# A row-normalising, row-doubling kernel: loads and stores in other groups, wide operations, roots on two engines

## The chip, the core and the metric

The kernel runs on one core of one Trainium2 chip. Times are microseconds of that core on the device. The core has a scalar engine (ScalarE, ACT in the profile), a vector engine (VectorE, DVE), a general engine (GpSimd, POOL), a tensor engine that this kernel doesn't use (PE), and a synchronising engine (SyncE, SP) that here only issues transfers. Sixteen DMA engines move the data between the chip's memory (HBM) and the on-chip memory (SBUF).

## What is computed

```python
x = randn(8, 512, 2048)   # float32
gamma = randn(2048)
x_rep = np.repeat(x, 2, axis=1)
rms = np.sqrt((x_rep ** 2).mean(axis=-1, keepdims=True) + 1e-6)
out = (x_rep / rms) * gamma
```

Every row of 2048 numbers is divided by the root of its mean square, multiplied by gamma, and written twice, one copy behind the other. The input is 4096 rows (33.6 MB), the output 8192 rows (67.1 MB).

## The kernel before

The 4096 rows are cut into 8 tiles of 128 partitions with K = 4 rows in each partition. A tile `y` has room for K * R = 8 rows per partition, R = 2: the four input rows are loaded into rows 4 to 7 (`at = K * (R - 1) + k`, line 51), and output row pairs 0-1, 2-3, 4-5, 6-7 are made in place from the front, so that an input row is overwritten only when it has been used. The pool `rows` has three such tiles, 64 KB per partition each. So three tiles can be in the works, and the load of tile i + 3 has to wait for the store of tile i.

For each row of a tile: `square` (line 61) has ACT square it and sum the squares along the way (line 64), and take the root of the mean (line 68); `scale` (line 71) has DVE take the reciprocal (line 73) and multiply row, reciprocal and gamma in one instruction into output row 2k (line 74); `repeat` (line 79) copies that to row 2k + 1, on ACT, or on DVE for the last row of a group (line 80). `compute` (line 82) puts these in an order in which ACT squares row k + 1 while DVE scales row k.

The order is written out by hand, and each engine runs its own instructions in the order in which the program gives them. The order on SP's queue is also that of the program: a `dma_start` that has to wait keeps those behind it waiting too. It is: load 0 in two halves, loads 1 and 2; then store 0, store 1, loads 3 and 4, store 2, store 3, loads 5 and 6, and so on in twos (lines 113 to 116). Tile 7 is loaded, computed and stored in halves (`parts`, line 108). Gamma is brought in by four small transfers from ACT's queue (line 98) and copied to all partitions by POOL (line 101).

Of the kernel before, what the change touches and what calls it, by code (L numbers as in the profile page):

```python
# [1 line left out]

# [4 lines left out]


@with_exitstack
def kernel(  # L10
    ctx: ExitStack,
    tc: tile.TileContext,
    x: bass.AP,
    gamma: bass.AP,
    out: bass.AP,
):
    nc = tc.nc
    P = nc.NUM_PARTITIONS
    f32 = mybir.dt.float32
    Act = mybir.ActivationFunctionType  # L20
    Alu = mybir.AluOpType

    B, S, D = x.shape
    Bo, So, Do = out.shape
    R = So // S
    assert R == 2 and D == Do and B == Bo and So == S * R
    eps = 1e-6
    inv_d = 1.0 / float(D)


    K = 4
    N = B * S
    assert N % (P * K) == 0
    ntiles = N // (P * K)
    x_t = x.rearrange("b s d -> (b s) d").rearrange("(n p k) d -> n p k d", p=P, k=K)
    out_t = out.rearrange("b s d -> (b s) d").rearrange("(n p j) d -> n p (j d)", p=P, j=K * R)

    singles = ctx.enter_context(tc.tile_pool(name="singles", bufs=1))
    rows = ctx.enter_context(tc.tile_pool(name="rows", bufs=3))
    junk = ctx.enter_context(tc.tile_pool(name="junk", bufs=1, space=bass.MemoryType.PSUM))  # L40
    small = ctx.enter_context(tc.tile_pool(name="small", bufs=8))

    ys = []

    def load(i, eng, parts=1):


        y = rows.tile([P, K * R, D], f32, name="y")
        step = K // parts
        for k in range(0, K, step):  # L50
            at = K * (R - 1) + k
            eng.dma_start(out=y[:, at : at + step, :], in_=x_t[i, :, k : k + step, :])  # L52
        ys.append(y)

    def store(i, k0, k1):
        nc.sync.dma_start(  # L56
            out=out_t[i, :, R * k0 * D : R * k1 * D],
            in_=ys[i][:, R * k0 : R * k1, :].rearrange("p j d -> p (j d)"),
        )

    def square(i, k):
        sq = junk.tile([P, D], f32, name="sq")
        ss = small.tile([P, 1], f32, name="ss")
        nc.scalar.activation(  # L64
            out=sq[:], in_=ys[i][:, K * (R - 1) + k, :], func=Act.Square, accum_out=ss[:]
        )
        rms = small.tile([P, 1], f32, name="rms")
        nc.scalar.activation(out=rms[:], in_=ss[:], func=Act.Sqrt, scale=inv_d, bias=eps_t[:])  # L68
        return rms

    def scale(i, k, rms):
        rstd = small.tile([P, 1], f32, name="rstd")
        nc.vector.reciprocal(out=rstd[:], in_=rms[:])  # L73
        nc.vector.scalar_tensor_tensor(  # L74
            out=ys[i][:, R * k, :], in0=ys[i][:, K * (R - 1) + k, :], scalar=rstd[:], in1=gamma_b[:],
            op0=Alu.mult, op1=Alu.mult,
        )

    def repeat(i, k, copy):
        copy(out=ys[i][:, R * k + 1, :], in_=ys[i][:, R * k, :])  # L80

    def compute(i, k0, k1):

        rms = square(i, k0)
        for k in range(k0, k1):
            scale(i, k, rms)
            if k + 1 < k1:
                rms = square(i, k + 1)
                repeat(i, k, nc.scalar.copy)
            else:  # L90
                repeat(i, k, nc.vector.tensor_copy)


    ctx.enter_context(tc.manual_schedule())
    load(0, nc.sync, parts=2)
    gamma_b = singles.tile([P, D], f32, name="gamma_b")
    for c in range(0, D, D // 4):
        nc.scalar.dma_start(
            out=gamma_b[0:1, c : c + D // 4], in_=gamma[c : c + D // 4].partition_broadcast(1)
        )  # L100
    nc.gpsimd.partition_broadcast(out_ap=gamma_b[:], in_ap=gamma_b[0:1, :])  # L101
    eps_t = singles.tile([P, 1], f32, name="eps_t")
    nc.vector.memset(eps_t, eps)  # L103
    load(1, nc.sync)
    load(2, nc.sync)

    for i in range(ntiles):
        parts = 2 if i == ntiles - 1 else 1
        for k in range(0, K, K // parts):
            compute(i, k, k + K // parts)  # L110
            store(i, k, k + K // parts)

        if i % 2 == 1:
            for j in (i + 2, i + 3):
                if j < ntiles:
                    load(j, nc.sync, parts=2 if j + 1 == ntiles else 1)


# [1 line left out]
_INS = ['x', 'gamma']  # L120
_OUTS = [((8, 1024, 2048), 'float32')]


# [23 lines left out]
```

## Time and profile before

| | |
|---|---|
| median of 10 runs | 239.82 us (239.68 to 240.98) |
| the profiled execution's own time | 239.77 us |
| its span, first to last instruction | 238.0 us |
| moved by DMA | 100.69 MB, 423 GB/s over the span |
| DVE, ACT, POOL busy | 90.8, 115.3, 2.5 us |
| DMA queue of loads and stores | 98.5% of 16 engines' span |

The profile is of one execution. A row such as "L74 DVE ... x32 | 75.3, 2352 | 1.2" says that line 74's instructions on DVE were 32, that they took 75.3 us together and 2352 ns each, and that DVE stood idle 1.2 us just before them. The chain of waits is followed back from the last instruction to whatever released it. "SPq" is the issue of a transfer on SP's queue; the time from issue to landing stands under "DMA". The slices cut the span into 40 equal parts, with the busy share of each in tenths.

### The profile page before, as it was taken

How to read it: one execution, taken by the hardware profiler on the slowest of the kernel's cores; microseconds unless marked ns; L12 is line 12 of the kernel's file. 1: busy time of each engine (PE TensorE's matmuls, PEld its weight loads, DVE VectorE, ACT ScalarE, POOL GpSimd, SP SyncE). 2: the span in 40 equal slices, each digit the busy share in tenths (PEclk: the TensorE clock that was granted, in tenths of full speed). 3: DMA queues.
4: the chain of work that ended last, by engine and by line, in shares of the span. 5: the costliest groups of instructions: out<-in, count | busy, mean ns of one | idle time of the engine just before them, and what ended most of it. 6: DMA issues, size and time to landing. Idle time of an engine off the chain costs nothing.

```text
span 238.0 us, 301 instructions
## 1 busy us (share of the span) xinstructions
DVE 90.8 (38%) x74; ACT 115.3 (48%) x121; POOL 2.5 (1%) x5
## 2 busy tenths in 40 slices
DVE  0086977864000084967000007796600009900000
ACT  2699999990000299996000049999400049700000
POOL 0300000000000000000000000000000000000000
DMA  7999998989899999989898999999898999898995
GB/s 262 441 443 441 441 441 352 529 352 518 364 408 430 435 408 436 529 352 529 352 529 352 435 424 464 441 408 474 352 529 352 410 435 531 386 474 364 430 430 242
DMA packets 2746, 100.69 MB, mean 423 GB/s; under 512 B 308, under 2 KB 308, under 8 KB 312
## 3 DMA queue, kind: packets, MB, share of 16 engines
q1 hardware_dynamic: 2736, 100.66, 98.5%
q14 instruction: 2, 0.02, 0.0%
q10 hardware_dynamic: 8, 0.01, 0.0%
HBM read 33.56 MB, written 67.11 MB: 423 GB/s over the span
## 4 chain that ended last, share of the span: by engine, by line
DMA 66%; ACT 15%; DVE 6%; issue 1%; SPq 0%; DVEq 0%
DMA out_dram<-y 40%; DMA y<-in_x_dram 25%; ACT sq L64 7%; ACT y L80 5%; DVE y L74 5%; ACT rms L68 1%; ACT L68 1%; DVE y L80 1%; DVE rstd L73 0%; SPq L52 0%; DVEq L74 0%; SPq L56 0%
## 5 line engine op out<-in xcount | busy, mean ns | idle before, releaser
L64 ACT ACTIVATE sq<-y 128x2048 f32<-128x2048 f32 x32 | 59.9, 1871 | 84.9 <-DMA y<-in_x_dram 84.9
L74 DVE SCALAR_TENSOR_TENSOR y<-y,rstd,gamma_b 128x2048 f32<-128x2048 f32 x32 | 75.3, 2352 | 1.2 <-DVE rstd L73 0.2
L73 DVE RECIPROCAL rstd<-rms 128x1 f32<-128x1 f32 x32 | 5.2, 162 | 115.7 <-ACT rms L68 115.7
L80 ACT COPY y<-y 128x2048 f32<-128x2048 f32 x23 | 43.4, 1888 | 3.7 <-DVE y L74 3.7
L80 DVE COPY y<-y 128x2048 f32<-128x2048 f32 x9 | 11.0, 1227 | 0.3
L68 ACT ACTIVATE rms<-ss,eps_t 128x1 f32<-128x1 f32 x32 | 9.4, 295 | 1.0
L64 ACT ACTIVATION_READ_ACCUMULATOR sq<-y 128x1 f32 x32 | 6.0, 186 | 0.0
L101 POOL PARTITION_BROADCAST gamma_b<-gamma_b x1 | 2.3, 2293 | 8.3 <-DMA gamma_b<-in_gamma_dram 8.3
L64 ACT ACT_TABLE_LOAD x1 | 1.3, 1283 | 2.1 <-issue 2.1
L68 ACT ACT_TABLE_LOAD x1 | 1.3, 1283 | 0.0
L103 DVE MEMSET eps_t<- 128x1 f32 x1 | 0.1, 59 | 0.8 <-PEq L131 0.8
L131 POOL MEMSET const-bfloat16-1.0<- 128x1 bf16 x1 | 0.1, 102 | 0.0
L131 POOL MEMSET const-uint8-127<- 128x1 uint8 x1 | 0.1, 101 | 0.0
L131 POOL MEMSET const-float32-0.0<- 128x1 f32 x1 | 0.1, 98 | 0.2 <-issue 0.2
L131 POOL MEMSET const-float32-1.0<- 128x1 f32 x1 | 0.1, 98 | 0.0
## 6 DMA issues: line engine op xcount, KB each, us to landing
y<-in_x_dram SPq DMA_DIRECT2D x6, 4096.0 KB, 25.0
y<-in_x_dram SPq DMA_DIRECT2D x4, 2048.0 KB, 9.6
out_dram<-y SPq DMA_DIRECT2D x2, 4096.0 KB, 26.8
out_dram<-y SPq DMA_DIRECT2D x7, 31.6
gamma_b<-in_gamma_dram ACTq DMA_DIRECT2D x4, 2.0 KB
```

Of the source, the lines that this page charges most:

```text
L64: nc.scalar.activation(out=sq[:], in_=ys[i][:, K * (R - 1) + k, :], func=Act.Square, accum_out=ss[:])
L68: nc.scalar.activation(out=rms[:], in_=ss[:], func=Act.Sqrt, scale=inv_d, bias=eps_t[:])
L73: nc.vector.reciprocal(out=rstd[:], in_=rms[:])
L74: nc.vector.scalar_tensor_tensor(out=ys[i][:, R * k, :], in0=ys[i][:, K * (R - 1) + k, :], scalar=rstd[:], in1=gamma_b[:], op0=Alu.mult, o ...
L80: copy(out=ys[i][:, R * k + 1, :], in_=ys[i][:, R * k, :])
L101: nc.gpsimd.partition_broadcast(out_ap=gamma_b[:], in_ap=gamma_b[0:1, :])
L103: nc.vector.memset(eps_t, eps)
L131: nc = _bacc.Bacc("TRN2", target_bir_lowering=False, num_devices=1)
```

## The change

The order on SP's queue becomes: first half of load 0, six pieces of gamma, second half of load 0, one more piece of gamma, loads 1 and 2; stores 0, 1, 2; loads 3, 4, 5; stores 3, 4; loads 6, 7; stores 5, 6, 7. Tile 7 is loaded, computed and stored whole, as are all others but the load of tile 0.

Most operations become wide: one instruction for several rows. `square` is now a plain square of several rows, written into output rows that are still free, and `reduce` has DVE sum them. In `mixed`, which does tiles 1, 2, 4, 6 and 7, ACT squares rows 1 to 3 of the tile in one instruction and row 0 with the sum (`total`), DVE reduces the three rows, `root` has POOL multiply, add and take the power -0.5 of all four sums, and DVE does the four multiplications with gamma; the copies are two instructions of two rows, one on ACT and one on DVE (both on ACT for tile 7). While DVE reduces tile i, ACT squares the whole of the next tile (`ahead`), for which DVE then reduces four rows (`row=False`). Tiles 0 and 3 take their roots in halves with ACT's square root and DVE's reciprocal (`root_quick`). Tile 5 is scaled by four ACT instructions, with the root as scale, and one wide multiplication by gamma on DVE; ACT copies all four rows.

Gamma's pieces go to two rows on partitions 0 and 32, and POOL spreads each half to all partitions by itself. ACT's table is loaded by `preload_act_table` ahead of the work.

```diff
-    def load(i, eng, parts=1):
...
+    def load(i, k0, k1):
         nc.sync.dma_start(
...
+            out=ys[i][:, K * (R - 1) + k0 : K * (R - 1) + k1, :], in_=x_t[i, :, k0:k1, :]
+        )
+
+    def store(i):
+        nc.sync.dma_start(out=out_t[i], in_=ys[i].rearrange("p j d -> p (j d)"))
...
+    def total(i, k, ss):
         sq = junk.tile([P, D], f32, name="sq")
...
+            out=sq[:], in_=ys[i][:, x_at + k, :], func=Act.Square, accum_out=ss[:, k : k + 1]
+        )
+
+    def square(i, k0, k1):
+
+        nc.scalar.activation(
+            out=ys[i][:, k0:k1, :], in_=ys[i][:, x_at + k0 : x_at + k1, :], func=Act.Square
+        )
+
+    def reduce(i, k0, k1, ss):
+        nc.vector.tensor_reduce(
+            out=ss[:, k0:k1], in_=ys[i][:, k0:k1, :], op=Alu.add, axis=mybir.AxisListType.X
+        )
+
+    def root(k0, k1, ss):
+        at = ss[:, k0:k1]
+        nc.gpsimd.tensor_scalar(
+            out=at, in0=at, scalar1=inv_d, scalar2=eps, op0=Alu.mult, op1=Alu.add
+        )
+        nc.gpsimd.tensor_tensor(out=at, in0=at, in1=power_t[:, k0:k1], op=Alu.pow)
+
+    def scale(i, k0, k1, rstd):
         for k in range(k0, k1):
...
+            nc.vector.scalar_tensor_tensor(
+                out=ys[i][:, R * k, :], in0=ys[i][:, x_at + k, :], scalar=rstd[:, k : k + 1],
+                in1=gamma_b[:], op0=Alu.mult, op1=Alu.mult,
+            )
+
+    def repeat(i, k0, k1, copy=nc.scalar.copy):
+        y_r = ys[i].rearrange("p (k r) d -> p k r d", r=R)
+        copy(out=y_r[:, k0:k1, 1, :], in_=y_r[:, k0:k1, 0, :])
...
+    cuts = [0, *range(D // 4, D + 1, D // 8)]
...
+    load(0, 0, H)
+    for c0, c1 in zip(cuts[:-2], cuts[1:-1]):
+        gamma_piece(c0, c1)
+    load(0, H, K)
+    gamma_piece(cuts[-2], cuts[-1])
+    for c0 in (0, D // 2):
+        nc.gpsimd.partition_broadcast(out_ap=gamma_b[:, c0 : c0 + D // 2], in_ap=gamma_half(c0))
+    load(1, 0, K)
+    load(2, 0, K)
...
+    def root_quick(k0, k1, ss):
+        at = ss[:, k0:k1]
+        nc.scalar.activation(out=at, in_=at, func=Act.Sqrt, scale=inv_d, bias=eps_t[:])
+        nc.vector.reciprocal(out=at, in_=at)
+
+    ss = columns()
+    for k in range(H):
+        total(0, k, ss)
+    root_quick(0, H, ss)
+    ss_b = columns()
+    between = ys[0].rearrange("p (k r) d -> p k r d", r=R)[:, 0:H, 1, :]
+    nc.scalar.activation(
+        out=between, in_=ys[0][:, x_at + H : x_at + K, :], func=Act.Square
+    )
+    scale(0, 0, H, ss)
+    nc.vector.tensor_reduce(
+        out=ss_b[:, H:K], in_=between, op=Alu.add, axis=mybir.AxisListType.X
+    )
+    root_quick(H, K, ss_b)
+    repeat(0, 0, H)
+    scale(0, H, K, ss_b)
+    repeat(0, H, K, nc.vector.tensor_copy)
+    store(0)
+
+    def mixed(i, ahead=None, last=nc.vector.tensor_copy, row=True):
+        ss = columns()
+        if row:
+            square(i, 1, K)
+            total(i, 0, ss)
+            reduce(i, 1, K, ss)
+        else:
+            reduce(i, 0, K, ss)
+        root(0, K, ss)
+        if ahead is not None:
+            square(ahead, 0, K)
+        scale(i, 0, K, ss)
+        repeat(i, 0, H)
+        repeat(i, H, K, last)
+        store(i)
+
+    mixed(1, ahead=2)
+    mixed(2, row=False)
+    for j in (3, 4, 5):
+        new_tile()
+        load(j, 0, K)
+    ss = columns()
+    for k in range(H):
+        total(3, k, ss)
+    root_quick(0, H, ss)
+    scale(3, 0, H, ss)
+    ss_b = columns()
+    for k in range(H, K):
+        total(3, k, ss_b)
+    root_quick(H, K, ss_b)
+    scale(3, H, K, ss_b)
+    repeat(3, 0, H)
+    repeat(3, H, K, nc.vector.tensor_copy)
+    store(3)
+    mixed(4, ahead=5)
+    for j in (6, 7):
+        new_tile()
+        load(j, 0, K)
+    ss = columns()
+    reduce(5, 0, K, ss)
+    root(0, K, ss)
+    for k in range(K):
+        nc.scalar.activation(
+            out=ys[5][:, R * k, :], in_=ys[5][:, x_at + k, :], func=Act.Copy, scale=ss[:, k : k + 1]
+        )
+    y_r = ys[5].rearrange("p (k r) d -> p k r d", r=R)
+    nc.vector.tensor_tensor(
+        out=y_r[:, :, 0, :], in0=y_r[:, :, 0, :],
+        in1=gamma_b[:].rearrange("p (k d) -> p k d", k=1).to_broadcast([P, K, D]), op=Alu.mult,
+    )
+    repeat(5, 0, K)
+    store(5)
+    mixed(6, ahead=7)
+    mixed(7, row=False, last=nc.scalar.copy)
```

## The prediction

> **What bounds the kernel now.** I read the page first: the busy shares, the slices and the DMA queue.
>
> ```profile
> span 238.0 us, 301 instructions
> DVE 90.8 (38%) x74; ACT 115.3 (48%) x121; POOL 2.5 (1%) x5
> DMA  7999998989899999989898999999898999898995
> ...
> q1 hardware_dynamic: 2736, 100.66, 98.5%
> ```
>
> No compute engine is busy for half the span; the DMA queue of the loads and stores is at work for 98.5% of it. So I asked the trace when it is not. Its packet records show 16 engines busy from 1.7 us to 235.8 us (the last ends at 236.77), and each packet size has one price: 0.611 us for 16 KB, 1.213 for 32 KB, 2.418 for 64 KB. A half load is 8 packets per engine of the first kind (4.89 us), a whole load 8 of the second (9.70), a whole store 8 of the third (19.34). Together 232.6 us per engine. The rest of the span is the start, a pause of 0.95 us that all engines show once, at 30 us, where the last load is followed by the first store, and the end. Transfers of the one queue run one behind the other, so only two things can change the time: the packets' sum, or a moment at which the queue is empty. For the second, the chain of waits:
>
> ```profile
> 26.55 26.07 DMA out_dram<-y
> 52.61 0.02 issue
> 52.63 28.96 DMA y<-in_x_dram
> ...
> 98.62 31.56 DMA out_dram<-y
> 130.19 0.02 issue
> 130.20 0.34 SPq L52
> 130.54 0.05 issue
> 130.59 0.03 SPq L56
> 130.62 0.03 issue
> 130.65 38.55 DMA out_dram<-y
> ```
>
> The reader is to see lead. The store of tile 0 is issued at 26.55, with loads ahead of it until about 32.5. Tile 3's is issued at 98.62, twelve microseconds before the store ahead of it has landed (110.8). Between them the engines are idle for 27 us at a stretch. This lead is what the change can spend. The rows that price it:
>
> ```profile
> L64 ACT ACTIVATE sq<-y 128x2048 f32<-128x2048 f32 x32 | 59.9, 1871 | 84.9 <-DMA y<-in_x_dram 84.9
> L74 DVE SCALAR_TENSOR_TENSOR y<-y,rstd,gamma_b 128x2048 f32<-128x2048 f32 x32 | 75.3, 2352 | 1.2 <-DVE rstd L73 0.2
> L73 DVE RECIPROCAL rstd<-rms 128x1 f32<-128x1 f32 x32 | 5.2, 162 | 115.7 <-ACT rms L68 115.7
> L80 DVE COPY y<-y 128x2048 f32<-128x2048 f32 x9 | 11.0, 1227 | 0.3
> L68 ACT ACTIVATE rms<-ss,eps_t 128x1 f32<-128x1 f32 x32 | 9.4, 295 | 1.0
> L101 POOL PARTITION_BROADCAST gamma_b<-gamma_b x1 | 2.3, 2293 | 8.3 <-DMA gamma_b<-in_gamma_dram 8.3
> L131 POOL MEMSET const-uint8-127<- 128x1 uint8 x1 | 0.1, 101 | 0.0
> ```
>
> **What the Trainium skill says.** "VectorE: DVE Perf Modes", section "The perf-mode tier table": an fp32 copy in SBUF moves two elements per cycle, tensor_reduce has one rate only, one per cycle. The copy row agrees: with the reciprocal's 0.16 us as the fixed part, (1227 - 162)/2047 = 0.52 ns per element, so one per cycle is 1.04 ns. No row shows a reduce. "DMA: Bandwidth & Descriptors", section "Anatomy of one DMA — SWDGE (gpsimd) path": a semaphore wait is made by the issuing sequencer before dispatch, not by the DMA engines. The waits of SP agree (its stores stood 121.4 us behind the copies of line 80). So one late store holds every load queued behind it.
>
> **The change part by part.** Times below are on the clock of the profiled execution, whose own time is 239.77 us at a span of 238.0; 1.77 us lie outside. That is 0.05 under the median of 239.82.
>
> *Packets.* Tile 7 is loaded and stored undivided: per engine 16 load packets of 0.611 become 8 of 1.213, and 16 store packets of 1.213 become 8 of 2.418: 0.07 + 0.07 us less. Gamma's pieces move to SP's queue: seven packets of under 0.09 us on one engine instead of four. The six pieces ahead of the second half of tile 0 delay its issue by some 6 x 0.35 us, hidden behind the first half, which runs until 7.3 us. The 1.28 us table load inside tile 0's chain goes. Sum on the queue: -0.13 us.
>
> *Prices for the wide operations.* Reduce of two, three, four rows: 4096, 6144, 8192 x 1.04 ns + 0.16 = 4.42, 6.55, 8.68 us. Wide DVE copy of two rows: 2.29. Wide squares of three and four rows: 0.833 ns per element + 0.17 ("ScalarE: Activation LUTs", section "What ACT_TABLE_LOAD costs"; the row of 1871 ns fits), 5.29 and 6.99. Four multiplies L74 in a row: starts 2.27 apart where nothing is waited for (12.10 to the next DVE start at 14.37), 2.38 where one waits for the one before, 9.3 to the end of the last.
>
> *Root on POOL.* Two instructions on 128x4, multiply-add and power, and three hand-overs. No row shows either. From below: two memsets' 0.10 and three hand-overs of 0.03 give 0.3. From above: "GPSIMD Engine Reference", section "Elementwise — side-by-side cycle accounting", has 2.6 cycles per element for a plain two-input add, and 12 for data-dependent branching; a power done by a loop in software may cost as much as the broadcast, 2.3. I take 0.8, since four columns are little work, and keep 0.3 to 2.3. DVE stands still all that time: it waits for the root with the multiplies queued behind.
>
> *Tile 0.* Squares 2.01 each from 8.14, sqrt, reciprocal: 12.65. But gamma's last piece lies behind the second half of tile 0 (lands 13.0), and half a broadcast is 1.2: first multiply at 14.55, not 12.10. Two multiplies to 19.1, reduce to 23.5, sqrt and reciprocal 24.05, two multiplies 28.8, copy 31.1: store 0 is issued at 31.2 instead of 26.55. The loads end at 31.75 (mean over engines, without the pause). A transfer into an empty queue begins later than its issue: the first load, issued at 0.72, has its first packets at 1.72 to 2.05, and they last 0.65 longer than the rest. I take 1.3 us, bounds 1.0 and 1.9. Start at 32.5: gap 0.7.
>
> *Tiles 1 and 2*, stores now back to back. ACT copies tile 0 (from 23.7, after sqrt) to 27.25, squares tile 1 to 32.5; DVE idles 1.5 us. Reduce 6.55 to 39.1, root 39.95, multiplies to 49.3, copy 51.6. Store 1 issued 51.65; store 0, with the pause, ends at 52.75: gap 0.15. Tile 2: reduce 8.68, root 0.8, multiplies 9.3, copy 2.3, with overlaps 21.1 from store to store: issued 72.7, wanted by 71.0: gap 1.7.
>
> *Tiles 3 to 5.* Loads 3 and 4 are issued only behind store 2, so they give no cover for it. Loads 3 to 5 run from 93.3 to 122.45; tile 3 (landed at 103.7) takes 16.4 on ACT and DVE: store 3 at 120.1, covered by load 5. Tile 4's reduce starts at 121.7 after ACT's copy and square; store 4 at 140.8, gap 0.3. Tile 5: reduce, root, four ACT scalings of 1.9, one wide multiply 8.68, one wide copy 6.99: issued 173.6, covered by loads 6 and 7 until 180.85.
>
> *Tiles 6 and 7.* ACT is free at 173.5; square, reduce 178.8 to 185.3, root, multiplies, copy: store 6 at 197.85, covered to 200.2. Tile 7: reduce 8.68, root, multiplies, ACT copy 3.58 instead of DVE's: store 7 at 220.2, begun 221.5, wanted 219.55: gap 1.95. Before, the halves of tile 7 were issued at 202.13 and 208.87 with the store of tile 6 in flight until 217, so the undivided tile gains nothing and exposes its whole chain.
>
> Sum: 0.7 + 0.15 + 1.7 + 0.3 + 1.95 = 4.8 (4.87 unrounded); 238.0 - 0.13 + 4.87 = 242.74; with 1.77, **244.5 us**, 2% slower. Each further microsecond of root adds six (five late stores, some twice); with 0.3 the sum is 241.5.
>
> **The rivals.**
> *The cover holds.* Tile 2's DVE chain has to come down from 21.1 to 19.3 us. If reduces take 0.85 of my price or less (or reduce and root share such a saving), no store is late and only the packets' sum is left: 239.77 - 0.13 = 239.65, no change. For it: DVE's sum in the page is 90.8 of 238 and even 137 would fit; my gaps are each under 2 us of a chain of 20. Against: the price follows from the copy row and the skill's table, and DVE alone is late for tiles 0 to 2. If the 0.95 us pause also went, 238.7. It decides from a store-to-store DVE time of 19.3.
> *The root is long.* At 2.0 us it is 251.7, at 1.5 us 248.7. For it: [...]POOL shows nothing like it; each of tiles 1, 2, 4, 6, 7 stops DVE for it. Against: four columns only.
>
> **How the numbers follow.** DVE paces the stores with a root of 0.3 to 1.3: chance 0.60, 241.5 to 247.5. Cover holds: 0.22, 238.7 to 240.3. Root long: 0.18, 247.5 to 260. Predicted 244.5. The range 239.5 to 251 leaves out the lower part of the second (0.06) and about half of the third. This kernel's time can be told from no change beyond 0.2%, 0.48 us: faster needs the pause gone, 0.06; same 0.16; slower 0.78.
>
> **What would show it.** Right: DMA slices with a dip near 32, 52, 73 and 220 us; SP's stores 1, 2 and 7 issued after the store ahead of them has ended, released by the copy; reduces of 6.55 and 8.68 us; a DVE wait of about 0.8 us for POOL. Wrong: DMA busy without a break from 2 to 236 us, or a POOL row over 1.5 us. It would also be wrong if a late store began well within 1 us of its issue.

## The result, and the profile after

| | before | after |
|---|---|---|
| median | 239.83 us | 249.05 us |
| ratio | | 1.0375, 95% interval 1.0364 to 1.0386 |
| span of the profiled execution | 238.0 us | 246.8 us |
| DVE, ACT, POOL busy | 90.8, 115.3, 2.5 us | 137.6, 103.7, 10.2 us |

The change makes the kernel 3.75% slower, 9.2 us. The page of after, its span, busy shares, slices and data queue:

```profile
span 246.8 us, 223 instructions
DVE 137.6 (56%) x46; ACT 103.7 (42%) x43; POOL 10.2 (4%) x20
DVE  0069977999890000019797996085047999780000
DMA  7999989959779796999997979799999989797893
q1 hardware_dynamic: 2462, 100.67, 95.9%
```

The queue's share fell from 98.5% of 238.0 us to 95.9% of 246.8. The slices have a 5 near 50 us, where the line of before has nothing below 8 between its ends. The many 7s say less: a slice counts packets where they begin, and with a full queue two or three rounds of 64 KB packets (2.418 us each) begin in a slice of 6.17 us. Two are 0.78 of it, a 7; in the slices of before, 5.95 us long, they are 0.81, an 8. So the holes below are read from the packet records and not from the slices. No engine is busy for much more than half of the span, and yet DVE sets the pace, because its work falls into the stretches in which one store follows another.

The issues of stores 0 and 1 were 14.8 us apart in before (26.55 and 41.34). In after, stores 1 and 2 are 21.6 us apart. Start and duration of the issue stand first; the line of before's store 1, then those of after's stores 1 and 2:

```profile
41.34 0.34 SPq L56 DMA_DIRECT2D out_dram<-y  x1
```

```profile
52.62 0.34 SPq L56 DMA_DIRECT2D out_dram<-y  x1
74.22 0.33 SPq L56 DMA_DIRECT2D out_dram<-y  x1
```

The timeline of after over tile 2 (start, duration, engine, line, operation; in brackets the idle time before it and who ended it):

```profile
50.26 2.29 DVE L94 COPY y<-y 128x4096 f32<-128x4096 f32 x1
52.47 8.68 DVE L74 TENSOR_REDUCE ss<-y 128x4 f32<-128x8192 f32 x1
61.23 0.19 POOL L80 TENSOR_SCALAR ss<-ss 128x4 f32<-128x4 f32 x1 [20.31 <-DVE ss L74]
61.51 1.01 POOL L83 TENSOR_TENSOR ss<-ss,power_t 128x4 f32<-128x4 f32 x1
62.56 9.26 DVE L87 SCALAR_TENSOR_TENSOR y<-y,ss,gamma_b 128x2048 f32<-128x2048 f32 x4 [1.41 <-POOL ss L83]
67.26 3.60 ACT L94 COPY y<-y 128x4096 f32<-128x4096 f32 x1 [17.99 <-DVE y L87]
71.86 2.29 DVE L94 COPY y<-y 128x4096 f32<-128x4096 f32 x1
74.65 21.70 SPq L51 DMA_DIRECT2D y<-in_x_dram  x3
```

From the copy of tile 1 (its end releases store 1) to the copy of tile 2 (its end releases store 2) DVE works with one pause, the 1.41 us of the root. That is the 21.6 us from store to store; a store keeps the DMA engines for 8 x 2.418 = 19.34 us. ACT had stood idle for 17.99 us when it got its copy. The loads are issued at 74.65 and after, behind store 2, so nothing else can fill the hole.

By the packet records the 16 engines were empty, on average, for 0.40 us ahead of store 0, 1.57 ahead of store 1, 2.18, 0.68 and 2.08 ahead of stores 2, 4 and 7: 6.9 us in sum. The records of before have no such hole. Besides, packets ran longer than is usual for their size by 3.9 us per engine in sum, against 1.7 before. 6.9 + 2.2 - 0.13 (fewer packets) = 9.0, against 8.8 in the spans.

The rows of after, shape by shape, for the new operations:

```profile
L87 DVE SCALAR_TENSOR_TENSOR y<-y,ss,gamma_b 128x2048 f32<-128x2048 f32 x28 | 64.8, 2350 | 9.8 <-POOL ss L83 7.4 <-POOL gamma_b L131 2.1
L74 DVE TENSOR_REDUCE ss<-y 128x4 f32<-128x8192 f32 x3 | 26.0, 8678 | 0.0
L74 DVE TENSOR_REDUCE ss<-y 128x3 f32<-128x6144 f32 x3 | 19.7, 6553 | 15.5 <-ACT y L69 15.5
L94 DVE COPY y<-y 128x4096 f32<-128x4096 f32 x6 | 13.8, 2294 | 0.2
L83 POOL TENSOR_TENSOR ss<-ss,power_t 128x4 f32<-128x4 f32 x6 | 6.1, 1017 | 0.5
L80 POOL TENSOR_SCALAR ss<-ss 128x4 f32<-128x4 f32 x6 | 1.2, 194 | 189.4 <-DVE ss L74 189.4
```

DVE's busy time grew by 46.8 us. The reduces of these two rows are 45.7, that of tile 0 another 4.4; what else DVE gained and lost (the wide multiplication of tile 5, fewer single multiplies and reciprocals) comes to 3.3 less. The 189.4 us of POOL cost nothing: it waits for work. The 7.4 us that DVE waited for POOL in five roots (1.48 each) do cost; the sixth root, tile 5's, is waited for by ACT.

### The profile page after: what moved, and what is told of

The parts are those of the page before. It is cut to its first block, busy times and chain, and to the rows that moved or that the text cites. A ratio compares the mean times of both kernels' runs of the same rounds, so it can differ in the third digit from the quotient of the medians.

```text
span 246.8 us, 223 instructions
## 1 busy us (share of the span) xinstructions
DVE 137.6 (56%) x46; ACT 103.7 (42%) x43; POOL 10.2 (4%) x20
## 3 DMA queue, kind: packets, MB, share of 16 engines
q1 hardware_dynamic: 2462, 100.67, 95.9%
## 5 line engine op out<-in xcount | busy, mean ns | idle before, releaser
L87 DVE SCALAR_TENSOR_TENSOR y<-y,ss,gamma_b 128x2048 f32<-128x2048 f32 x28 | 64.8, 2350 | 9.8 <-POOL ss L83 7.4
L94 ACT COPY y<-y 128x4096 f32<-128x4096 f32 (+1 forms) x9 | 35.8, 3982 | 56.6 <-DVE y L87 47.9
L74 DVE TENSOR_REDUCE ss<-y 128x3 f32<-128x6144 f32 (+1 forms) x6 | 45.7, 7616 | 15.5 <-ACT y L69 15.5
L69 ACT ACTIVATE y<-y 128x6144 f32<-128x6144 f32 (+1 forms) x6 | 37.0, 6168 | 1.6 <-DMA y<-in_x_dram 1.6
L63 ACT ACTIVATE sq<-y 128x2048 f32<-128x2048 f32 x9 | 16.8, 1872 | 41.0 <-DMA y<-in_x_dram 40.9
L94 DVE COPY y<-y 128x4096 f32<-128x4096 f32 x6 | 13.8, 2294 | 0.2
L211 DVE TENSOR_TENSOR y<-y,gamma_b 128x8192 f32<-128x8192 f32 x1 | 8.7, 8693 | 9.3 <-ACT y L207 9.3
L207 ACT ACTIVATE y<-y,ss 128x2048 f32<-128x2048 f32 x4 | 7.8, 1994 | 13.3 <-POOL ss L83 13.3
L80 POOL TENSOR_SCALAR ss<-ss 128x4 f32<-128x4 f32 x6 | 1.2, 194 | 189.4 <-DVE ss L74 189.4
L83 POOL TENSOR_TENSOR ss<-ss,power_t 128x4 f32<-128x4 f32 x6 | 6.1, 1017 | 0.5
L156 DVE TENSOR_REDUCE ss<-y 128x2 f32<-128x4096 f32 x1 | 4.4, 4414 | 0.0
```

Source lines behind the costliest of these rows:

```text
L63: nc.scalar.activation(out=sq[:], in_=ys[i][:, x_at + k, :], func=Act.Square, accum_out=ss[:, k : k + 1])
L69: nc.scalar.activation(out=ys[i][:, k0:k1, :], in_=ys[i][:, x_at + k0 : x_at + k1, :], func=Act.Square)
L74: nc.vector.tensor_reduce(out=ss[:, k0:k1], in_=ys[i][:, k0:k1, :], op=Alu.add, axis=mybir.AxisListType.X)
L83: nc.gpsimd.tensor_tensor(out=at, in0=at, in1=power_t[:, k0:k1], op=Alu.pow)
L87: nc.vector.scalar_tensor_tensor(out=ys[i][:, R * k, :], in0=ys[i][:, x_at + k, :], scalar=rstd[:, k : k + 1], in1=gamma_b[:], op0=Alu.mul ...
L94: copy(out=y_r[:, k0:k1, 1, :], in_=y_r[:, k0:k1, 0, :])
```

## The experiments

Each is compared with the kernel before on the same chip: 239.9 us for the first four, 240.02 for the others. Theory A is that DVE's chain from store to store makes stores late; rival B, that the new order on the queue costs the time by itself; rival C, that all other lateness is inherited from tile 0.

| run | what it is | time, us | ratio to before |
|---|---|---|---|
| e1_root_act | roots on ACT and DVE | 243.66 | 1.0158 (1.0143 to 1.0173) |
| e2_order | before with the new queue order | 240.35 | 1.0029 (1.0014 to 1.0043) |
| e3_quick_all | no POOL root, no reduce but tile 0's | 240.41 | 1.0018 (1.0009 to 1.0028) |
| e4_cover | loads 3 and 4 ahead of store 2 | 248.24 | 1.0352 (1.0334 to 1.0369) |
| e5_halves | tile 7 stored in halves | 247.10 | 1.0297 (1.0281 to 1.0313) |
| e6_root_long | a second power in each root | 255.10 | 1.0637 (1.0622 to 1.0653) |
| e7_whole7 | before with tile 7 whole | 240.19 | 1.0009 (1.0001 to 1.0017) |
| e8_pairs | e3 with order and gamma of before | 239.72 | 0.9994 (0.9981 to 1.0008) |

### The root made shorter

```diff
-        root(0, K, ss)
+        root_quick(0, K, ss)
         if ahead is not None:
...
-    root(0, K, ss)
+    root_quick(0, K, ss)
     for k in range(K):
```

> Of the changed kernel, only the roots of tiles 1, 2, 4, 5, 6, 7 move: ScalarE's square root and VectorE's reciprocal instead of GpSimd's two instructions, with the square of the next tile behind them on ScalarE. Theory A (VectorE's chain from store to store paces the late stores, and the root stands in it): a root costs 0.55 us instead of 1.4 to 1.6, stores 1, 2, 4 and 7 are each late by some 0.9 less, 244 to 245 us. Rival B (the order of the queue itself costs the time, by changes of direction and by loads that come too late): 248 to 249.

The timeline of this run over tile 2:

```profile
51.16 8.68 DVE L74 TENSOR_REDUCE ss<-y 128x4 f32<-128x8192 f32 x1
59.87 0.30 ACT L143 ACTIVATE ss<-ss,eps_t 128x4 f32<-128x4 f32 x1 [10.05 <-DVE ss L74]
60.20 0.18 DVE L144 RECIPROCAL ss<-ss 128x4 f32<-128x4 f32 x1 [0.36 <-ACT ss L143]
60.41 9.26 DVE L87 SCALAR_TENSOR_TENSOR y<-y,ss,gamma_b 128x2048 f32<-128x2048 f32 x4
```

From the reduce's end at 59.84 to the first multiply pass 0.57 us instead of 1.41; at tile 1 it is 0.64 instead of 1.60. The time fell by 5.4 us, to 243.66, just below the 244 to 245 that were expected: the empty time of the packet records went from 7.3 us in all, start and end included, to 3.2; store 4 and store 7 are no longer late. With the square of the next tile now behind the root on ACT, DVE still found it done. The longer packets stayed (3.4 us).

### The root made longer

```diff
         nc.gpsimd.tensor_tensor(out=at, in0=at, in1=power_t[:, k0:k1], op=Alu.pow)
+        nc.gpsimd.tensor_tensor(out=at, in0=at, in1=one_t[:, k0:k1], op=Alu.pow)
...
+    one_t = singles.tile([P, K], f32, name="one_t")
+    nc.gpsimd.memset(one_t, 1.0)
```

> The changed kernel with a second power, by 1.0, behind each root on GpSimd: about 1.05 us more on each of six roots. Theory A: the stores 1, 2, 4, 6 and 7 are later by five to six times that: 254 to 255.5. Rival (the root is hidden behind other work in most tiles): 249 to 251.

Measured 255.10. The rows of POOL in this run:

```profile
L83 POOL TENSOR_TENSOR ss<-ss,power_t 128x4 f32<-128x4 f32 x6 | 6.1, 1016 | 0.5
L84 POOL TENSOR_TENSOR ss<-ss,one_t 128x4 f32<-128x4 f32 x6 | 6.0, 1007 | 0.5
```

Store 1 is issued at 53.61 instead of 52.62, store 2 at 76.29 instead of 74.22: each root adds 1.04 us to the chain. The time rose by 6.05 us, 5.8 for each microsecond of root; e1_root_act gave 5.4 for 0.84 to 0.96, about 6. All six roots pass their length on, tile 5's too, though loads cover store 5: ACT gets to the square of tile 6 only when it is done with tile 5, and DVE's reduce of tile 6 waits for that square. That reduce in the changed kernel, then in this run:

```profile
182.30 6.55 DVE L74 TENSOR_REDUCE ss<-y 128x3 f32<-128x6144 f32 x1 [12.31 <-ACT y L69]
```

```profile
186.63 6.55 DVE L74 TENSOR_REDUCE ss<-y 128x3 f32<-128x6144 f32 x1 [12.31 <-ACT y L69]
```

It starts 4.33 us later, four roots' worth. Store 6 is then issued 5.41 us later (207.40 instead of 201.99), store 7 6.49 us later (231.35 instead of 224.86).

### The order alone, and the wide work alone

e2_order changes only the loop that issues the loads in the kernel before:

```diff
-        if i % 2 == 1:
-            for j in (i + 2, i + 3):
-                if j < ntiles:
-                    load(j, nc.sync, parts=2 if j + 1 == ntiles else 1)
+        for j in {2: (3, 4, 5), 4: (6, 7)}.get(i, ()):
+            load(j, nc.sync, parts=2 if j + 1 == ntiles else 1)
```

> The kernel before with the new grouping on SP's queue alone: stores 0, 1, 2, loads 3, 4, 5, stores 3, 4, loads 6, 7, stores 5, 6, 7; tile 7 stays in halves, all operations narrow as before. Theory A: its stores are ready every 15 us, so none is late: 239.5 to 240.3. Rival B: 243 or more, most of the loss. In between (241 to 242.5) if the order brings only the longer packets, 2.2 us of them in the changed kernel's trace.

e3_quick_all keeps the new order and all else, but does each of tiles 1 to 7 as the changed kernel does tile 3:

```diff
+    def quick(i):
+        ss = columns()
+        for k in range(H):
+            total(i, k, ss)
+        root_quick(0, H, ss)
+        scale(i, 0, H, ss)
...
+        repeat(i, 0, H)
+        repeat(i, H, K, nc.vector.tensor_copy)
+        store(i)
...
-    mixed(1, ahead=2)
-    mixed(2, row=False)
+    quick(1)
+    quick(2)
```

> The changed kernel with tiles 1, 2, 4, 5, 6 and 7 done the way it does tile 3: squares with sums on ScalarE, square root there, reciprocal, multiplies and wide copy on VectorE; no reduce on VectorE but in tile 0, no root on GpSimd. Queue order, tile 0, gamma and undivided tile 7 as changed. Theory A: VectorE needs 12 us from store to store instead of 19 to 21.6, only store 0 can be late (0.4 us): 239.5 to 241, up to 242 if the longer packets stay. Rival B: 246 or more. Rival C (tile 0's late start is what all others inherit): 246 or more too, with stores 1 and 2 late.

The pages of e2_order and then of e3_quick_all, busy shares, DMA slices and queue:

```profile
DVE 90.8 (38%) x74; ACT 115.2 (48%) x121; POOL 2.5 (1%) x5
DMA  7999998989898998999998989899998999999996
q1 hardware_dynamic: 2736, 100.66, 98.6%
```

```profile
DVE 99.2 (42%) x57; ACT 97.2 (41%) x86; POOL 2.9 (1%) x8
DMA  7999998989898998999998998989999998989894
q1 hardware_dynamic: 2462, 100.67, 98.5%
```

Both have the whole queue back. The order alone costs 0.45 us (ratio 1.0029), just above what was expected, and has no hole anywhere; its packets ran longer by 2.5 us in sum against 1.7. It isn't what makes the changed kernel slow. In e3_quick_all the wide copies, gamma on SP's queue and the undivided tile are all there; store 0 is late by 0.4 us, as in the changed kernel, and its lateness is not passed on, since stores 1 and 2 are issued 12.75 us apart:

```profile
43.70 0.34 SPq L56 DMA_DIRECT2D out_dram<-y  x1
56.45 0.33 SPq L56 DMA_DIRECT2D out_dram<-y  x1
```

So rival C falls too. The step from e1_root_act to e3_quick_all is worth another 3.25 us. It takes away the reduces of tiles 1, 2 and 4 to 7, and with them the wide squares, tile 5's own way and tile 7's second copy on ACT; the share of the reduces alone was not measured. Together with the root's 5.4 us this is all but 0.5 us of the loss.

One pairing was not tried: the wide work of the changed kernel in the queue order of before, where two loads follow every two stores. So it is shown that the order alone costs 0.45 us, but not how much of the 9.2 us the wide work would cost without it.

### Cover from two loads

```diff
     mixed(1, ahead=2)
-    mixed(2, row=False)
-    for j in (3, 4, 5):
+    for j in (3, 4):
         new_tile()
         load(j, 0, K)
+    mixed(2, row=False)
+    new_tile()
+    load(5, 0, K)
```

> The changed kernel with loads 3 and 4 put ahead of store 2 on the queue; nothing else moves. Theory A: the loads (19.4 us) cover tile 2, and tile 4 starts earlier, so that stores 2 and 4 are no longer late; stores 1 and 7 still are: 245 to 246. Rival B: no gain, 248.5 to 249.5, or a loss by one more change of direction.

Measured 248.24: 0.8 us won where 3 to 4 were expected. The part about the stores was right: stores 2 and 4 found the queue full. But SP's issues show what I had not counted:

```profile
53.73 21.63 SPq L51 DMA_DIRECT2D y<-in_x_dram  x2
75.46 0.38 SPq L56 DMA_DIRECT2D out_dram<-y  x1
114.70 0.33 SPq L51 DMA_DIRECT2D y<-in_x_dram  x1
115.13 23.83 SPq L56 DMA_DIRECT2D out_dram<-y  x2
```

Load 5 needs the buffer of tile 2 and so waits for store 2 to land; now store 2 is the last transfer in the queue, and store 3 stands behind load 5 on SP, though tile 3 was copied by 101.2 us. The queue runs empty: the windows of 112 to 118 us show it, for this run and then for the changed kernel (DVE, ACT, POOL busy, clock, DMA share, GB/s):

```profile
112.00:118.00 6.00, 5.96 (x4) 0.00 (x0) 0.00 (x0) 1.00 0.50 169
```

```profile
112.00:118.00 6.00, 5.93 (x5) 5.34 (x4) 0.00 (x0) 1.00 1.01 437
```

By the packet records the engines are empty for 1.9 us there, and packets run longer around it by some 1.7. One hole was closed and another opened. Store 7 and store 1 stayed late (1.3 and 1.7 us). For theory A this run is half a confirmation: cover takes a late store away, but most of the gain was lost to a wait that I had overlooked. By its time alone, 248.24, it stands nearer to rival B's 248.5 than to A's 246.

### The last tile

```diff
-    mixed(7, row=False, last=nc.scalar.copy)
+    ss = columns()
+    reduce(7, 0, K, ss)
+    root(0, K, ss)
+    half = K * R // 2
+    for h, copy in ((0, nc.scalar.copy), (1, nc.vector.tensor_copy)):
+        scale(7, h * H, (h + 1) * H, ss)
+        repeat(7, h * H, (h + 1) * H, copy)
+        nc.sync.dma_start(
+            out=out_t[7][:, h * half * D : (h + 1) * half * D],
+            in_=ys[7][:, h * half : (h + 1) * half, :].rearrange("p j d -> p (j d)"),
+        )
```

> The changed kernel with tile 7 finished in halves: two rows scaled, copied on ScalarE and stored, then the other two, copied on VectorE and stored. Theory A: the first half is ready near 220.3, before store 6 ends at 222.8, the second near 223.6 with the first in flight; the 2.1 us hole ahead of the last store goes: 246.9 to 247.3. Rival (what is late in the end is inherited from earlier stores, and the division changes nothing): 248.5 to 249.3.

Measured 247.10, 1.95 us less. SP's issues after 202 us: in this run

```profile
202.40 0.34 SPq L56 DMA_DIRECT2D out_dram<-y  x1
220.67 3.62 SPq L225 DMA_DIRECT2D out_dram<-y  x2
```

and in the changed kernel store 7 at 224.86. The first half's store, four microseconds earlier, finds store 6 in flight. (The second half's copy also moved from ACT to DVE, 2.29 us instead of 3.60.) e7_whole7 is the opposite trial, the undivided tile in the kernel before (`parts = 1` at line 108 and in line 116):

> The kernel before with tile 7 loaded, computed and stored whole. The prediction's count of packets gives 0.13 us less and no late store, since tile 7 is ready in some 16 us while 21 us of store 6 are still to run: 239.6 to 239.9, not told from before. Rival (the undivided tile always exposes its chain): 241 or more.

It took 240.19 against 240.02, a ratio of 1.0009 (1.0001 to 1.0017). Less was expected, 239.6 to 239.9; the 0.13 us of fewer packets did not show. There tile 7 is stored at 215.5, after 171.93 for tile 6, with the queue full. So the undivided last tile cost at most 0.4 us where its work was done early, and 2 us where it wasn't.

### Putting it together

e8_pairs takes the loads and stores of e3_quick_all in the order of before, and gamma as before:

```diff
...
-    quick(1)
-    quick(2)
-    for j in (3, 4, 5):
-        new_tile()
-        load(j, 0, K)
...
+    for i in range(1, ntiles):
+        quick(i)
+        if i % 2 == 1:
+            for j in (i + 2, i + 3):
+                if j < ntiles:
+                    new_tile()
+                    load(j, 0, K)
```

> The kernel of run e3_quick_all with the loads and stores in the order of before and gamma on ScalarE's queue as before; tile 7 whole. VectorE needs 12 us from store to store and store 0 is issued near 29, ahead of the end of the loads: no hole, 239.4 to 239.9. If the grouping in threes is what lengthens packets in e2_order and e3_quick_all by some 0.5 us, that goes too. Rival (wide operations cost by themselves): 240.3 or more.

It took 239.72 us, 0.9994 of before (0.9981 to 1.0008): no difference. Wide copies and fewer instructions neither helped nor harmed this kernel, which is bound by its transfers. Its packets ran longer by 1.5 us in sum, less than with stores in threes (2.1), but that is one profile of each.

## Why the prediction was right, and what was mis-sized

The mechanism and the direction were right: DVE paces the stores, and the late ones are those that were named. The size was not: 4.7 us of loss were forecast and 9.2 measured, 244.5 and 249.05 us, within the range to 251. By the prediction's own division it is not the likeliest case that came (root of 0.3 to 1.3 us, 241.5 to 247.5) but the rival "the root is long" (247.5 to 260), which had a chance of 0.18. Both rest on the same chain.

- **Packets' sum.** The time of a packet of each size stayed as counted; the 0.13 us can't be seen beside the rest, and e7_whole7 did not show it.
- **Prices of the wide operations.** Reduces 6.55 and 8.68, wide copy 2.29, four multiplies 9.3 were forecast; 6.553, 8.678, 2.294 and 9.26 were measured. What the Trainium skill's page "VectorE: DVE Perf Modes" states in "The perf-mode tier table", one element per cycle for tensor_reduce, is thereby seen in this case: (8678 - 6553)/2048 = 1.04 ns per element, twice the copy's 0.52. The wide squares took 5.32 and 7.02 us for 5.29 and 6.99.
- **Root on POOL.** This is the term that was mis-sized. I took 0.8 us, hand-overs included, from no row at all; DVE stood for 1.41 to 1.60 us, above the 1.3 of the likeliest case. The power alone is 1.007 us on four columns, five times the multiply-add beside it (0.19). The lever of six microseconds per microsecond of root was right: 5.8 and about 6 in the two runs that turned it. By that lever 0.6 us too little is worth some 3.5 us.
- **How the 4.5 us come together.** In the profiles the span is 4.0 us over the forecast 242.74: the holes are 2.1 us larger (6.9 for 4.87), and longer packets add 2.2. The last 0.5 us is that the profiled execution (248.56) was faster than the median. So the holes grew by less than the root's 3.5 us, because other terms leaned the other way; they are named below.
- **Tile 0.** Store 0 was forecast for 31.2 and issued at 31.42, with gamma as the cause of the late first multiply: 14.55 forecast, 14.78 measured, DVE released by POOL's second broadcast. Its hole was 0.40, not 0.7.
- **Late stores.** Stores 1, 2, 4 and 7 were forecast late by 0.15, 1.7, 0.3 and 1.95, and were by 1.57, 2.18, 0.68 and 2.08. Stores 3, 5 and 6 were covered, as forecast. Two of the sum's other terms leaned the other way. A store into the empty queue has its first packets 0.82 to 0.86 us after its issue (52.62 to 53.46), not 1.3: outside my bounds of 1.0 to 1.9, and within the 1 us that I had named as a sign of being wrong. And the longer packets delay a store's end, so that the chain behind it is late by less.
- **The pause.** I carried one pause of 0.95 us over from before. The changed kernel has none at store 0, but has packets longer by 0.8 to 1.0 us at three other changes of direction: store 2 to load 3, store 4 to load 6, load 7 to store 5. All longer packets together are 2.2 us more than before, the other part of the miss. I had not foreseen it, and its cause is open.
- **The rivals.** That the cover holds fell: it needed 19.3 us from store to store, and the chain has 21.6. A run with less than its 19.3, e3_quick_all with 12.75, does keep the queue full behind store 0. That the root is long is what happened: 1.5 us was priced at 248.7, and 1.41 to 1.60 gave 249.05. That these agree so well is in part luck, since that price has starts that are too late and lacks the longer packets, and the two nearly cancel. Its sign, a POOL row over 1.5 us, did not come: the longest was 1.06, and the wait is two rows and their hand-overs.

## What to carry to other kernels

In a kernel bound by its transfers, an engine that is half idle over the whole can still set the time, as DVE did here at 56%: compare its chain from one store to the next (21.6 us) with the duration of a store (19.34), in the stretch in which stores follow each other. A small operation on a third engine in the midst of that chain can cost its whole length once per tile; here each microsecond of the root was worth about six. Grouping transfers in one direction leaves fewer loads between stores to cover such a chain; that this mattered here follows from the order and was not tested by itself. A load that waits for the last transfer in the queue to land opens a hole by itself, 1.9 us in e4_cover.

## What was not expected of the hardware

Nearly all packets of one size take one time to a few nanoseconds: 1.213 us for 32 KB, in loads and in the half stores of before alike, and 2.418 for the 64 KB of whole stores. The exceptions are the very first packets (about 0.6 us longer), those after the hole in e4_cover, and some changes between loads and stores, where packets on most or all of the 16 engines run longer by 0.5 to 1.1 us. Before had one such place (load 2 to store 0, 0.95 us); the changed kernel three; e2_order 1.08 at load 2 to store 0 and 0.59 at load 7 to store 5. They recur at the same changes in the profiles of kernels with the same order (store 2 to load 3: 0.8, 0.8, 0.8 and 1.0 us in the changed kernel, e1_root_act, e5_halves and e6_root_long), but many changes have none, and no run here tells what decides it.
